# First layer's value projection as seven block products instead of eight, spread between the q and k projections

## The chip, the cores and the metric

The kernel runs on one core of one Trainium2 chip. The metric is the device time of one execution in microseconds (us); the median of two executions of the kernel before is 1992.58 us (1992.47 to 1992.68). A core has TensorE (PE, matrix products, with its weight loads shown apart as PEld), VectorE (DVE), ScalarE (ACT), GpSimd (POOL) and SyncE (SP, which issues most of the transfers). Each engine works through its own list of instructions in order.

## The reference, cut to what matters

Two layers over 256 tokens of width 2048, in float32. The change lies in the token mixer of the first layer (12 heads of width 128, plus 4 heads into 256 memory tokens):

```python
n = rms_norm(h, attn_norm[i])
z = n @ a_w_in[j]                                   # 2048 x (3*1536 + 512)
q, k, v, qm = jnp.split(z, [MIX_WIDTH, 2 * MIX_WIDTH, 3 * MIX_WIDTH], axis=-1)
mix = neighbourhood_attention(split_heads(q, 12), split_heads(k, 12), split_heads(v, 12), a_rpb[j])
km, vm = jnp.split(m @ w_mem_kv[i], 2, axis=-1)
cross = memory_attention(split_heads(qm, 4), split_heads(km, 4), split_heads(vm, 4))
h = h + jnp.concatenate([mix, cross], axis=-1) @ w_o[i]
n = rms_norm(h, mlp_norm[i])
h = h + jnp.square(jax.nn.relu(n @ w_up[i])) @ w_down[i]
```

The value projection is v = n @ (columns 3072 to 4607 of a_w_in): 256 x 2048 times 2048 x 1536.

## The kernel before

Every float32 operand of a large product is split into two rounded parts, hi (ScalarE copies it into the rounded type, L457) and lo (VectorE subtracts hi from the source, L458), and each product is three matmuls: hi times hi, hi times lo, lo times hi.

Weights come in chunks of 128 x 2048 floats (1 MB) into a ring: three buffers `raw` for what arrives, four `hi` and four `lo` tiles of half a chunk each (`new_half`). There are two kinds of chunk:

- kind "S" (`add_s`, `products`, L363): one head of 128 columns over all 2048 rows. The weights are the stationary operand, the 256 tokens are the moving one, so a matmul has 256 columns; 24 matmuls a half. The result is feature by token. Queries, keys and memory queries of the first layer and the MLP's up projection (`ps_u`) are of this kind.
- kind "M" (`add_m`, `m_products`, L340, L343, L344): 512 output columns over 512 rows. The tokens are stationary (two tiles of 128), the weights move, so a matmul has 512 columns; 12 matmuls a half. Values, w_o and the second layer's projections are of this kind.

`plan` is a list of chunks. `run_all` turns it into grains of half a chunk, calls the preparing stages a few grains ahead (`ahead`), and runs the grain; `later(n, fn)` puts a piece of work n grains after the present one. A scheduler then orders the instructions of each engine, from which the engines' lists come.

In the first layer the plan has four memory queries, and then three times: four chunks of values (512 columns, four heads) followed by the q and k chunks of those four heads. After each k chunk a narrow ("near") head starts: scores of 160 keys per token tile (`attend_near`), the turning of the probabilities through VectorE and SP's DMAs (`turned_near`), their split, and the product with the values (`attend3_near`). The memory heads go through `attend`, `turned`, `halved`, `attend3`. Values are read from PSUM, scaled and split by `put_values`.

The MLP already has a seven-product form for its down projection (`down_grains`): sums of the four weight blocks, made by VectorE and one accumulating DMA from the POOL queue (L1118 to L1124), and sums of the activations.

The starting places of operands are set by hand, in bytes: an S half starts `STILL_AT` = 64 bytes into its `hi` and `lo` tiles, an M half at byte 0, and a ring tile is longer than its 1024 floats by `LONGER`. The first S half behind an M half has its first 128 columns of lo elsewhere in the tile (`entered_half`, `Entered`).

Of the kernel before, what the change touches and what calls it, by code (L numbers as in the profile page):

```python
# [17 lines left out]
P = 128  # L18
# [41 lines left out]
LONGER = {"hi": 128, "lo": 128}  # L60
# [89 lines left out]

class Grain:


# [5 lines left out]
def encoder_kernel(ctx: ExitStack, tc: tile.TileContext, t: dict, out: bass.AP):  # L159
# [23 lines left out]
    def open_sums(layer=1):  # L183

        for x in ("acc", "att")[:: 1 if layer else -1]:
            setattr(at, x, opened(f"ps_{x}", space=bass.MemoryType.PSUM, bufs=4))

    def open_ring():
        at.ring = opened("ring")
        at.cat = opened("cat")  # L190

        for pool in (at.ring, at.cat):
            pool.tile([P, 64], F32, tag="pad", name="pad")
# [3 lines left out]

    open_sums()
    open_ring()
    open_work()  # L200

    first = const.tile([P, GAINS + NT * D], F32, name="first")
    gains, mem0 = first[:, :GAINS], first[:, GAINS:]
    h = mem0.rearrange("p (a b) -> p a b", a=NT)
# [3 lines left out]
    def load_mem(j):  # L210
        s = slice(GAINS + j * 512 if j else 0, GAINS + (j + 1) * 512)
        nc.sync.dma_start(first[:, s], t["mem_rest"][j - 1] if j else t["mem_first"])
# [26 lines left out]
    def gain(which, k):  # L239
        return gains[:, which * KT + k : which * KT + k + 1]  # L240
# [127 lines left out]
    def begin():  # L368

        box["memT"] = at.cat.tile([P, KT, 512], F32R, tag="cat", name="memT")  # L370
        tiles = {}
# [126 lines left out]
    def summed(ps, name, row, factor=1.0):  # L498

        s = at.work.tile([P, SEQ], F32, tag="sum_s", name=f"{name}_s")  # L500
        nc.vector.scalar_tensor_tensor(s, ps, factor, row, op0=ALU.mult, op1=ALU.mult)
        return s


    def attend(qT, kT):
# [19 lines left out]
        for s in range(NT):  # L525
            if box["layer"]:
                nc.scalar.activation(sc[:, s, :], sc[:, s, :], AF.Copy, scale=rs[:, s : s + 1])
            else:
                nc.vector.tensor_scalar(sc[:, s, :], sc[:, s, :], rs[:, s : s + 1], None, op0=ALU.mult)
        return sc  # L530

    def attend2(sc):
        pt = at.att.tile([P, NT, SEQ], F32, tag="att", name="pt_a")
        for s in range(NT):
            i = NT - 1 - s
            for k in range(NT):
                nc.tensor.transpose(pt[:, k, i * P : (i + 1) * P], sc[:, s, k * P : (k + 1) * P], ident)
        pT = at.work.tile([P, 2, NT, SEQ], F32R, tag="pT", bufs=2 + box["layer"], name="pT")
        return pT, split(pT[:, 0], pT[:, 1], pt)
# [20 lines left out]
    def turned(sc):  # L560
# [7 lines left out]
        pT = at.work.tile([P, 2, 4, NT, NT * 32], F32R, tag="pT", bufs=2 + box["layer"], name="pT_t")  # L568
# [55 lines left out]
    def attend3_near(pT, v, head, cat):  # L624
# [14 lines left out]
        y = at.work.tile([P, SEQ], F32, tag="av_s", name="av_s")  # L639
# [71 lines left out]
    def head_of(v, hd):  # L711
        return lambda part, kt: v[:, part, kt, hd * HD : (hd + 1) * HD]
# [32 lines left out]
    def vm_done(layer):  # L745
        def f(w):
# [4 lines left out]
            for i in range(NT):  # L751
                v = at.work.tile([P, 2, 512], F32R, tag="pT", name="vm_w")
# [22 lines left out]
    mem_sq = at.work.tile([P, 512], F32, tag="b_o", bufs=3, name="mem_sq")  # L775
# [20 lines left out]
    def x_load():  # L796
        box["xT"] = []
        for a in range(2):
            y = at.work.tile([P, 8, SEQ], F32, tag="l4", name="xT")
            pin(nc.sync.dma_start(y.rearrange("p a b -> p (a b)"), t["xT"][:, a * XW // 2 : (a + 1) * XW // 2]))  # L800
            box["xT"].append(y)
# [15 lines left out]
    def x_norm(j):  # L817
        if j == 0:
            box["nT"] = wide("nT0", 480)
        for k in (2 * j, 2 * j + 1):  # L820
            split_pair(box["nT"], box["xT"][k // 8][:, k % 8, :], G_A0, k)
# [21 lines left out]
    def a_k_done(hd):  # L843
        def f(w):
# [5 lines left out]
            attention([(box.pop(("q", hd)), k, b, head_of(box["v", hd // GH], hd % GH), hd, box["cat"])], 1,  # L850
                      steps=(0, 1, 3, 4 if hd == NH - 1 else 8 if hd % GH == GH - 1 else 7))
        return f

    def a_qm_done(hd):
        def f(w):
# [6 lines left out]
            attention([(q, box["km"][:, hd, :], None, head_of(box["vm"], hd), NH + hd, box["cat"])], 1)  # L862
# [30 lines left out]
    def o_done(layer, nb):  # L893
# [41 lines left out]
        def f(w):  # L935
            if nb == 0:
                closed("work")
# [288 lines left out]
    def plain_grains(layer, nb, at_chunk):  # L1226
# [19 lines left out]
        def begin():  # L1246
            if nb == REST[0]:
                closed("ps_sums")
                open_sums(layer)
# [295 lines left out]
    for j in range(8):  # L1545
        later(24 + j, x_norm, j)
    later(28, x_stats)
# [28 lines left out]
def m_chunks(w):  # L1576

    k, n = w.shape
    x = w.reshape(k // D, 4, 4, P, n // 512, 512).transpose(0, 4, 1, 3, 2, 5)
    return np.ascontiguousarray(x).reshape(-1, P, CH)  # L1580
# [118 lines left out]
```

## Time and profile before

| what | value |
|---|---|
| median of the executions | 1992.58 us |
| the profiled execution's own time | 1992.26 us |
| its span in the profile | 1990.3 us, 32806 instructions |
| TensorE busy | 1981.8 us, 100%, 12838 matmuls |
| VectorE busy | 1716.2 us, 86% |
| ScalarE busy | 1340.0 us, 67% |
| GpSimd busy | 138.3 us, 7% |
| moved by DMA | 448.52 MB, mean 225 GB/s |

The span is what the profiler saw from the first instruction to the last; the execution's own time is 1.96 us longer. A matmul's bar in the profile is 276 to 278 ns long at 256 columns and about 390 ns at 512, but the next one starts long before it ends, so the cost of a matmul is read from one start to the next, not from its bar. For VectorE and ScalarE a bar also overlaps its neighbour a little when both wait for nothing.

### The profile page before, as it was taken

The numbers are of one execution on the slowest core, as the hardware profiler recorded it, in microseconds if no ns is written. First come the engines' busy times: TensorE is split into PE (matmuls) and PEld (weight loads), VectorE is DVE, ScalarE is ACT, GpSimd is POOL, SyncE is SP. The second block draws the span as 40 slices with busy tenths as digits, with TensorE's granted clock in tenths as the row PEclk, the third lists the DMA queues.
The fourth block names the chain that finished last, engine by engine and source line by source line (L and its number), as shares of the span: only waits on it lengthen the run. The fifth ranks groups of instructions, "written<-read, shape, count | busy, mean of one in ns | idle before, by whom it ended". The sixth has DMA issues, their size and how long they took to land.

```text
span 1990.3 us, 32806 instructions
## 1 busy us (share of the span) xinstructions
PE 1981.8 (100%) x12838; PEld 1800.0 (90%) x12838; DVE 1716.2 (86%) x2131; ACT 1340.0 (67%) x1892; POOL 138.3 (7%) x179
## 2 busy tenths in 40 slices
PE   9999999999999999999999999999999999999998
PEld 8999999899999999999998888889999999999997
DVE  7777777588898999999999778788998999999998
ACT  6655555477777777777766658677776777777674
POOL 0000000000000000000000001000000000000000
PEclk9999999999999999999999999999999999999999
DMA  8856655767777777777766765667777777777772
GB/s 293 321 194 202 206 189 184 271 191 234 239 230 227 232 236 238 230 228 235 216 229 198 259 223 182 211 213 251 236 224 236 226 226 238 234 238 229 225 236 105
DMA packets 117339, 448.52 MB, mean 225 GB/s; under 512 B 24640, under 2 KB 49984, under 8 KB 69824
## 3 DMA queue, kind: packets, MB, share of 16 engines
q1 hardware_dynamic: 99168, 415.12, 59.6%
q0 software_dynamic: 17728, 30.78, 9.7%
q8 instruction: 101, 1.65, 0.3%
q10 hardware_dynamic: 288, 0.52, 0.1%
q14 instruction: 54, 0.44, 0.1%
HBM read 397.78 MB, written 4.19 MB: 202 GB/s over the span
## 4 chain that ended last, share of the span: by engine, by line
PE 99%; issue 0%; DMA 0%; ACT 0%; DVE 0%; DVEq 0%; POOLq 0%; POOL 0%; SPq 0%; ACTq 0%
PE ps_u L363 35%; PE ps_s L363 10%; PE p L1152 9%; PE p L1150 9%; PE p L1153 9%; PE ps_m L344 8%; PE ps_m L340 8%; PE ps_m L343 8%; PE sc_ps L514 0%; PE av L655 0%; PE sc_ps L513 0%; PE sc_ps L515 0%; PE av L654 0%; PE av L656 0%; PE av L630 0%
## 5 line engine op out<-in xcount | busy, mean ns | idle before, releaser
L363 PE MATMUL ps_u<-hT,uh 128*128 128x256 f32 x3812 | 663.9, 276 | 0.0
L363 PEld LDWEIGHTS ps_u<-hT,uh 128*128 128x128 f32 x3812 | 579.1, 188 | 5.5
L363 PE MATMUL ps_u<-hT,ul 128*128 128x256 f32 x1960 | 541.7, 276 | 0.0
L457 ACT ACTIVATE uh<-raw_U 128x1024 fp32r<-128x1024 f32 x262 | 276.8, 1058 | 210.1 <-PE ps_u L363 194.7
L363 PEld LDWEIGHTS ps_u<-hT,ul 128*128 128x128 f32 x1960 | 368.2, 188 | 0.0
L458 DVE TENSOR_TENSOR lo<-raw,hi 128x1024 fp32r<-128x1024 f32 (+1 forms) x215 | 254.0, 1187 | 93.6 <-ACT hi L457 92.7
L458 DVE TENSOR_TENSOR ul<-raw_U,uh 128x1024 fp32r<-128x1024 f32 x262 | 318.1, 1217 | 17.3 <-ACT uh L457 17.3
L458 DVE TENSOR_TENSOR tl<-t,th 128x2048 fp32r<-128x2048 f32 x116 | 265.5, 2289 | 71.0 <-ACT th L457 70.6
L457 ACT ACTIVATE hi<-raw 128x1024 fp32r<-128x1024 f32 (+1 forms) x215 | 222.1, 1039 | 140.7 <-PE ps_m L344 72.9
L457 ACT ACTIVATE th<-t 128x2048 fp32r<-128x2048 f32 x116 | 222.7, 1919 | 118.0 <-PE p L1153 114.9
L458 DVE TENSOR_TENSOR bl<-b,bh 128x1536 fp32r<-128x1536 f32 x116 | 203.1, 1751 | 0.0
L1150 PE MATMUL p<-th,a_s 128*128 128x512 f32 x464 | 181.2, 391 | 0.0
L1152 PE MATMUL p<-tl,a_s 128*128 128x512 f32 x464 | 181.0, 390 | 0.0
L1153 PE MATMUL p<-th,a_s 128*128 128x512 f32 x464 | 180.5, 389 | 0.0
L1119 POOL DMA_DIRECT2D t<-b x116 | 100.7, 868 | 1142.0 <-ACT t L1118 1059.7
L457 ACT ACTIVATE bh<-b 128x1536 fp32r<-128x1536 f32 x116 | 172.3, 1486 | 7.9
L363 PE MATMUL ps_s<-nT,hi 128*128 128x256 f32 x896 | 154.7, 277 | 0.0
L1153 PE MATMUL p<-bh,a_s 128*128 128x512 f32 x348 | 136.2, 391 | 0.0
L1152 PE MATMUL p<-bl,a_s 128*128 128x512 f32 x348 | 135.7, 390 | 0.0
L363 PEld LDWEIGHTS ps_s<-nT,hi 128*128 128x128 f32 x896 | 135.6, 188 | 0.1
L1150 PE MATMUL p<-bh,a_s 128*128 128x512 f32 x348 | 135.4, 389 | 0.0
L363 PE MATMUL ps_s<-nT,lo 128*128 128x256 f32 x448 | 124.1, 277 | 0.0
(303 smaller groups left out, 3585.6 us busy)
## 6 DMA issues: line engine op xcount, KB each, us to landing
raw_U<-in_w_up SPq DMA_DIRECT2D x128, 1024.0 KB, 6.0
b<-in_w_pair SPq DMA_DIRECT2D x116, 1024.0 KB, 5.8
raw<-in_w_o SPq DMA_DIRECT2D x32, 1024.0 KB, 5.1
t<-b POOLq DMA_DIRECT2D x116, 256.0 KB, 5.2
raw<-in_w_b SPq DMA_DIRECT2D x21, 1024.0 KB, 5.7
raw<-in_w_av SPq DMA_DIRECT2D x12, 1024.0 KB, 5.0
raw<-in_w_aq SPq DMA_DIRECT2D x12, 1024.0 KB, 4.9
raw<-in_w_ak SPq DMA_DIRECT2D x12, 1024.0 KB, 5.0
```

The costliest lines, as they stand in the source:

```text
L340: first = nc.tensor.matmul(ps, ah, hi[:, s], start=st, stop=False)
L343: nc.tensor.matmul(ps, ah, lo[:, s], start=False, stop=False)
L344: final = nc.tensor.matmul(ps, al, hi[:, s], start=False, stop=sp)
L363: ins = nc.tensor.matmul(ps, x, acts[:, k, part], start=k == n == 0, stop=k == KT - 1 and n == 2)
L457: first = nc.scalar.activation(dst_hi, src, AF.Copy)
L458: return first, nc.vector.tensor_tensor(dst_lo, src, dst_hi.bitcast(F32), op=ALU.subtract)
L1119: nc.gpsimd.dma_start(s[:, 3, :], b[:, 1, :], accum_op=ALU.add)
L1150: ins = nc.tensor.matmul(ps, a[:, 0, ai, :], hi[:, s], start=begins, stop=False)
L1152: nc.tensor.matmul(ps, a[:, 0, ai, :], lo[:, s], start=False, stop=False)
L1153: nc.tensor.matmul(ps, a[:, 1, ai, :], hi[:, s], start=False, stop=ends)
```

## The change

The values of four heads (512 columns) are now computed from 2 x 2 blocks: the two token tiles of 128, pairs of 128-row blocks of the weights, and halves of 256 columns. Seven products per pair of blocks, each 128 tokens by 256 columns, take the place of eight. That needs sums of the activations (`x_sums`, made once, in `left`, in part of `cat` and in the room of h, which is loaded a second time after the values are done) and sums of the weights (`value_grains`: one ScalarE copy, two VectorE additions and two accumulating DMAs from the POOL queue for each of the 12 chunks). The seven sums stand in four PSUM banks, and seven VectorE additions (`values_done`, three times) make the four blocks of values from them.

The plan no longer has values in blocks of four chunks. One value grain follows each of the 28 projection chunks (four memory queries, then q and k of each head) from the third on, which is the third memory query, and two follow n = 4, 5 and 6 (the first head's q and k and the second head's q), until the 24 grains are used up. Beside them the q and k products alternate between the two halves of one PSUM bank (`"turns"`); PSUM then has five `acc` and three `att` banks in the first layer, four and four before. The ring tiles become shorter to make room: `hi` by 112 floats, `lo` by 64. Several work tiles lose a buffer. The memory heads' probabilities are scaled by ScalarE instead of VectorE, and their steps stand further apart.

```diff
-LONGER = {"hi": 128, "lo": 128}
+LONGER = {"hi": 16, "lo": 64}
...
-        for x in ("acc", "att")[:: 1 if layer else -1]:
-            setattr(at, x, opened(f"ps_{x}", space=bass.MemoryType.PSUM, bufs=4))
+        for x, n in (("acc", 5 - layer), ("att", 3 + layer))[:: 1 if layer else -1]:
+            setattr(at, x, opened(f"ps_{x}", space=bass.MemoryType.PSUM, bufs=n))
...
+            if place == "turns":
+                if "turns" not in box:
+                    box["turns"] = [0, at.acc.tile([P, 512], F32, tag="acc", name="ps_s")]
+                box["turns"][0] += 1
+                w.ps = box["turns"][1][:, box["turns"][0] % 2 * SEQ :][:, :SEQ]
+                return
...
+    def x_sums(c):
...
+        d = at.work.tile([P, 2, 4, P], F32, tag="pT", bufs=1, name="x_d")
+        for n, a, b, op in ((0, x[:, :, 0], x[:, :, 2], ALU.subtract), (1, x[:, :, 0], x[:, :, 1], ALU.add),
+                            (2, d[:, :, 0], x[:, :, 1], ALU.add), (3, x[:, :, 3], d[:, :, 2], ALU.subtract)):
+            nc.vector.tensor_tensor(d[:, :, n], a, b, op=op)
+        split(res[:, :, 0], res[:, :, 1], d)
...
-    def a_v_done(g):
-        def f(w):
-            box["v", g] = values("l4", "va")
-            put_values(box["v", g], w.ps, box["x_col"])
-        return f
+    PARTS = (("p3", "p1", "p2", "p7"), ("p6", "p4", "p5"))
...
+        def pre():
+            b = own["b"].rearrange("p (a b) -> p a b", a=4)
+            s = own["t"] = at.spare.tile([P, 4, 512], F32, tag="sums", name="v_t")
+            nc.scalar.activation(s[:, 2:4, :], b[:, 2:4, :], AF.Copy)
+            nc.vector.tensor_tensor(s[:, 0, :], b[:, 3, :], b[:, 0, :], op=ALU.add)
+            nc.gpsimd.dma_start(s[:, 3, :], b[:, 1, :], accum_op=ALU.add)
+            nc.vector.tensor_tensor(s[:, 1, :], s[:, 0, :], b[:, 1, :], op=ALU.add)
+            nc.gpsimd.dma_start(s[:, 2, :], s[:, 1, :], accum_op=ALU.add)
+
+        def prep(n):
+            b, s = own["b"], own["t"].rearrange("p a b -> p (a b)")
+            for m, src in enumerate(((s[:, 512 : 1536], s[:, 1536:]) if n else (b[:, :HALF], b[:, HALF : 1536], s[:, :512]))):
+                if m < 2:
+                    own[n, m] = new_half("S")
+                at_ = slice(0, src.shape[-1]) if m < 2 else slice(512, HALF)
+                split(*(x[:, at_] for x in own[n, min(m, 1)]), src)
...
+        def run(n):
...
+                        for part, x, st, sp in ((0, hi, begin and half == 0, False), (0, lo, False, False),
+                                                (1, hi, False, end)):
...
+                            ins = nc.tensor.matmul(ps, ah, x[:, s], start=st, stop=sp, skip_group_check=True)
...
+    def values_done(g):
...
+        nc.scalar.activation(c[:, 0, 0], p["p1"], AF.Copy)
+        for d, x, y, op in ((c[:, 1, 0], p["p2"], c[:, 0, 0], ALU.add), (c[:, 1, 1], p["p6"], c[:, 0, 0], ALU.subtract),
+                            (c[:, 0, 1], c[:, 1, 1], p["p7"], ALU.subtract), (c[:, 0, 0], c[:, 0, 1], p["p4"], ALU.add),
+                            (c[:, 0, 1], p["p5"], c[:, 0, 1], ALU.subtract),
+                            (c[:, 1, 1], c[:, 1, 1], p["p5"], ALU.subtract), (c[:, 1, 1], c[:, 1, 1], p["p3"], ALU.add)):
+            nc.vector.tensor_tensor(d, x, y, op=op)
...
-    for hd in range(NMH):
-        add_s(t["w_aqm"][hd], get("nT"), a_qm_done(hd))
-    for g in range(NH // GH):
-        add_m([t["w_av"][g * 4 + c] for c in range(4)], parts_of("nT"), a_v_done(g))
-        for hd in range(g * GH, (g + 1) * GH):
-            add_s(t["w_aq"][hd], get("nT"), a_q_done(hd))
-            add_s(t["w_ak"][hd], get("nT"), a_k_done(hd))
+    CHUNKS = (2, 0, 1, 3)
+    with_values = [x for g in range(NH // GH) for n, c in enumerate(CHUNKS) for x in value_grains(g, c, n == 0, n == 3)]
+    projections = [(t["w_aqm"][hd], a_qm_done(hd)) for hd in range(NMH)]
+    for hd in range(NH):
+        projections += [(t["w_aq"][hd], a_q_done(hd)), (t["w_ak"][hd], a_k_done(hd))]
+    for n, (src, done) in enumerate(projections):
+        add_s(src, get("nT"), done, "turns" if with_values else None)
+        for _ in range((n > 1) + (n in (4, 5, 6))):
+            if with_values:
+                plan.append(with_values.pop(0))
```

What this makes of the lists of instructions is seen at two places. On TensorE, where the first values are computed, behind a memory head (`av`, `sc_ps`), before and then now; `ps_m` and `ps_v` are the values' sums, `nT` the normed tokens, `left` their sums:

```order
L656 MATMUL av<-pT_t,vm 128x256
L340 MATMUL ps_m<-hi,nT_920 128x512
L343 MATMUL ps_m<-lo,nT_920 128x512
L344 MATMUL ps_m<-hi,nT_920 128x512
L340 MATMUL ps_m<-hi,nT_920 128x512
L343 MATMUL ps_m<-lo,nT_920 128x512
```

```order
L540 MATMUL sc_ps<-km,qmT 128x256
L928 MATMUL ps_v<-hi,left 128x256
L928 MATMUL ps_v<-lo,left 128x256
L928 MATMUL ps_v<-hi,left 128x256
L928 MATMUL ps_v<-hi,nT_925 128x256
L928 MATMUL ps_v<-lo,nT_925 128x256
```

288 matmuls of 512 columns are gone, 504 of 256 columns stand in their place, in groups of 24 and 18 between the q and k products (`ps_s`), which before came without a break.

On VectorE, where the last two memory heads (`nm`, `sc_t`, `pT_t`) are worked on while the first values are prepared, before:

```order
L524 RECIPROCAL rs<-sm 128x2
L529 TENSOR_SCALAR sc<-sc,rs 128x256 x2
L566 STREAM_TRANSPOSE sc_t<-sc 128x2x4x32 x2
L458 TENSOR_TENSOR lo<-raw,hi 128x1024 x2
L458 TENSOR_TENSOR cat_1154<-av,cat_1154 128x256
L458 TENSOR_TENSOR pT_t<-pT_t 128x512
L314 TENSOR_TENSOR lo<-raw,hi 128x128
L314 TENSOR_TENSOR lo<-raw,hi 128x896
L458 TENSOR_TENSOR lo<-raw,hi 128x1024 x2
```

and now (`v_t` are the weight sums, `x_d` and `cat<-x_d` the last of the activation sums):

```order
L894 TENSOR_TENSOR v_t<-raw 128x512
L332 TENSOR_TENSOR lo<-raw,hi 128x896
L588 STREAM_TRANSPOSE sc_t<-sc 128x2x4x32 x2
L896 TENSOR_TENSOR v_t<-v_t,raw 128x512
L544 TENSOR_REDUCE nm<-sc_ps 128x2
L526 SCALAR_TENSOR_TENSOR qm_s<-ps_s,x_row 128x256
L483 TENSOR_TENSOR cat_1177<-x_d,cat_1177 128x2x512
L483 TENSOR_TENSOR lo<-raw,hi 128x1024
L549 RECIPROCAL rs<-sm 128x2
L483 TENSOR_TENSOR qmT<-qm_s,qmT 128x256
L483 TENSOR_TENSOR lo<-raw,hi 128x1024
L588 STREAM_TRANSPOSE sc_t<-sc 128x2x4x32 x2
```

The memory heads, the sums of activations and weights and the splits of three kinds of chunk now share one stretch of VectorE's list.

More of the change, by code (lines that the diff above doesn't have):

```diff
@@ L370, in begin @@
         box["memT"] = at.cat.tile([P, KT, 512], F32R, tag="cat", name="memT")
+        later(1, lambda: nc.scalar.activation(gains, first[:, LEFT : LEFT + GAINS], AF.Copy))
         tiles = {}
@@ new lines, in values_done @@
+    def values_done(g):
+        p = {name: box["v_ps"][bank][:, half * SEQ : (half + 1) * SEQ] for name, (bank, half) in PLACES.items()}
+        c = at.work.tile([P, NT, 2, SEQ], F32, tag="pT", bufs=1, name="v_c")
+        nc.scalar.activation(c[:, 0, 0], p["p1"], AF.Copy)
[4 more added lines that the diff above has]
+            nc.vector.tensor_tensor(d, x, y, op=op)
+        box["v", g] = values("l4", "va")
+        put_values(box["v", g], [c[:, i].rearrange("p a b -> p (a b)") for i in range(NT)], box["x_col"])
+        if g == NH // GH - 1:
+            h_load()
@@ L936, in f @@
             if nb == 0:
+                if not layer:
+                    closed("spare")
                 closed("work")
@@ L1544, in encoder_kernel @@
     later(21, x_load)
[L1545 to L1547 removed]
+    for n, j in enumerate((4, 5, 0, 1, 2, 3, 6, 7)):
+        later(24 + n, x_norm, j)
+    for n, c in zip((28, 30, 32, 35), CHUNKS):
+        later(n, x_sums, c)
+    later(26, x_stats)
     run_all()
```

130 lines of the change are left out of this document (100 added, 30 removed).

## The prediction

> **What bounds the kernel now.** I read the busy times first, then the slices, then the chain of work that ended last.
>
> ```profile
> PE 1981.8 (100%) x12838; PEld 1800.0 (90%) x12838; DVE 1716.2 (86%) x2131; ACT 1340.0 (67%) x1892; POOL 138.3 (7%) x179
> PE   9999999999999999999999999999999999999998
> DVE  7777777588898999999999778788998999999998
> PEclk9999999999999999999999999999999999999999
> PE 99%; issue 0%; DMA 0%; ACT 0%; DVE 0%; DVEq 0%; POOLq 0%; POOL 0%; SPq 0%; ACTq 0%
> ```
>
> TensorE is busy throughout, its granted clock never drops, and the chain is 99% TensorE. So only two things move the time: what a matmul costs from one start to the next, and a new wait of TensorE. VectorE is the next engine, 70 to 80% busy in the slices of the first layer's projections (a slice is 49.8 us). The busy times of each engine in three stretches of that stage say it more closely (sum, then the number of instructions):
>
> ```profile
> core 0: us, PE busy (x) PEld busy (x) DVE busy (x) ACT busy (x) POOL busy (x), PEclk, DMA share, GB/s
> 94.00:330.00 236.00, 236.00 (x1769) 224.29 (x1768) 178.11 (x340) 123.81 (x212) 10.97 (x22) 1.00 0.61 202
> 105.50:156.50 51.00, 51.00 (x353) 47.06 (x351) 37.90 (x61) 27.54 (x48) 0.00 (x0) 1.00 0.58 193
> ```
>
> From 94 to 330 us TensorE has no gap, VectorE works 178.1 us of 236, ScalarE 123.8. The transfers are at 0.61 of their engines, so loading the same weights in another order, and h twice (two transfers more on SP's list of some 600), I cost at nothing; a late 1 MB chunk would show as an idle `hi` copy.
>
> **The change part by part: the matmuls.** First the chain, then TensorE's own rows, give the cost from start to start.
>
> ```profile
> 213.54 14.52 PE ps_s L363 x128
> ...
> 204.70 0.39 PE L340 MATMUL ps_m<-hi,nT 128*128 128x512 f32 x1
> ...
> 211.95 0.39 PE L344 MATMUL ps_m<-hi,nT 128*128 128x512 f32 x1
> ...
> L340 PE MATMUL ps_m<-hi,nT 128*128 128x512 f32 x96 | 37.5, 390 | 0.0
> L343 PE MATMUL ps_m<-lo,nT 128*128 128x512 f32 x96 | 37.4, 390 | 0.0
> L344 PE MATMUL ps_m<-hi,nT 128*128 128x512 f32 x96 | 37.6, 391 | 0.0
> ```
>
> 128 matmuls of 256 columns in 14.52 us are 113.4 ns each. The two 512-column rows are 32 matmuls apart: 7.25 us / 32 = 226.6 ns, twice 113.3, so two narrow ones cost what a wide one does. Removed are the three groups, 288 x 226.6 ns = 65.3 us; with slower ones at each switch of kind the starts add up to 65.7. Added are 504 (12 chunks, 42 each) x 113.4 = 57.2 us. **Gain 8.5 us.** The other bound is the nearest row of a product of the tokens-stationary kind that really has 256 columns, the kernel's last products:
>
> ```profile
> 1977.26 0.28 PE L343 MATMUL ps_m<-ul,a_s 128*128 128x256 f32 x1
> ...
> 1981.94 0.28 PE L343 MATMUL ps_m<-l_p,a_p 128*128 128x256 f32 x1
> ```
>
> Those are 39 matmuls apart, 4.68 / 39 = 120.0 ns; 504 x 120.0 = 60.5, a gain of 5.2. I take 8.5 here and put the difference into the next term, because I think I know where it comes from.
>
> [...]
>
> **The starting places.** In the kernel before, the `hi` tiles lie (1024 + 128) x 4 = 4608 bytes apart, 36 times 128. Now it is (1024 + 16) x 4 = 4160, 32.5 times 128, so every second `hi` tile starts 64 bytes off its old place modulo 128. Before, every q and k matmul reads its moving operand 64 bytes, modulo 128, from the next one's weights, and the last products, 120.0 ns each, read them 0 apart. Counting addresses through the new program, 544 of 1695 narrow pairs of the S kind and 177 of 498 value pairs become 0 apart, and 483 of 1758 wide pairs 64 apart. At 120.0 − 113.4 = 6.6 ns that is 3.6 + 1.2 = 4.8 us, and another 0 to 3.2 if the wide ones suffer too: bounds 0 to 8. But one row speaks against laying it all on the place:
>
> ```profile
> 422.18 17.91 PE ps_u L363 x152
> ```
>
> These 152 narrow matmuls also have operands 64 apart and still take 117.8 ns, so only 120.0 − 117.8 = 2.2 ns is surely left for the place: 721 x 2.2 = 1.6 us. Between 1.6 and 4.8 I take **+2.6 us**, nearer to the 117.8, since that row stands in a far longer run than the 4.7 us of the last products.
>
> **VectorE's share.** What an operation costs when VectorE waits for nothing is read from starts:
>
> ```profile
> 601.13 1.08 DVE L458 TENSOR_TENSOR a_s<-c,a_s 128x896 fp32r<-128x896 f32 x1
> 602.13 1.75 DVE L458 TENSOR_TENSOR bl<-b,bh 128x1536 fp32r<-128x1536 f32 x1
> 603.80 0.69 DVE L1122 TENSOR_TENSOR t<-b 128x512 f32<-128x512 f32 x1
> 604.40 1.22 DVE L458 TENSOR_TENSOR ul<-raw_U,uh 128x1024 fp32r<-128x1024 f32 x1
> 605.54 0.68 DVE L1123 TENSOR_TENSOR t<-t,b 128x512 f32<-128x512 f32 x1
> 606.14 1.22 DVE L458 TENSOR_TENSOR ul<-raw_U,uh 128x1024 fp32r<-128x1024 f32 x1
> ...
> 173.08 0.41 DVE L501 SCALAR_TENSOR_TENSOR q_s<-ps_s,x_row 128x256 f32<-128x256 f32 x1
> 173.41 0.47 DVE L590 TENSOR_REDUCE nm<-sc 128x2 f32<-128x320 f32 x1
> ```
>
> So 896 elements take 1.00 us, 512 take 0.60, 1024 take 1.14, 256 about 0.33; on the same line 128 would be 0.20, and an entered half (128 + 896) 1.20. By the two lists the change takes away 30 splits of 1024 (−34.2) and the scaling of the memory heads (−2.4, ScalarE does it now); it adds 18 entered halves (21.6), per value chunk one raw split of 512, one split of a sum of 1024 and two of 512 and two additions of 512 (12 x 4.14 = 49.7), 21 additions that make the values (7.0), and the activation sums (16 x 0.33 + 4 x 1.14 = 9.9); splitting the normed tokens in pairs saves 1.1. Together +50.5 us: 178.1 + 50.5 = 228.6 against TensorE's 236 − 8.5 = 227.5. ScalarE gets some 45 more and stays under 75%.
>
> This is not even. Where one grain follows each projection VectorE's list has 16.0 us of work per head, TensorE 138 matmuls (15.6 us) and 1.1 for the head itself, 16.7, so it holds. Between the first value product and the end of the doubled places (n = 4, 5, 6) TensorE has 51 us of work, and VectorE's list holds 63: 13 splits of 1024, 14 of 512 and 6 entered halves (30.4), 8 weight sums (4.8), activation sums (6.4), the values' additions (3.0), near heads and q, k (5.4), and most of the four memory heads (12.8), whose steps and scaling before are these:
>
> ```profile
> L566 DVE STREAM_TRANSPOSE sc_t<-sc 128x256 f32<-128x256 f32 x8 | 4.6, 614 | 0.0
> L519 DVE TENSOR_REDUCE nm<-sc_ps 128x2 f32<-128x512 f32 x4 | 2.8, 688 | 1.4 <-PE sc_ps L515 1.4
> L458 DVE TENSOR_TENSOR pT_t<-pT_t 128x512 fp32r<-128x512 f32 x4 | 2.8, 692 | 4.4 <-ACT pT_t L457 4.4
> L501 DVE SCALAR_TENSOR_TENSOR qm_s<-ps_s,x_row 128x256 f32<-128x256 f32 x4 | 1.7, 418 | 0.5 <-PE ps_s L363 0.5
> L529 DVE TENSOR_SCALAR sc<-sc,rs 128x256 f32<-128x256 f32 x8 | 2.4, 347 | 0.0
> ```
>
> Less 0.08 us of overlap a bar, a head's two transposes, maximum, split of pT_t, and three steps of 256 elements (qm_s and two more) are 2 x 0.53 + 2 x 0.61 + 3 x 0.34 = 3.3 us, four heads 13.2. The 63 us are 12 too many. VectorE enters with a lead, which the ring bounds: a tile becomes free, ScalarE copies, VectorE subtracts, TensorE uses it.
>
> ```profile
> 99.77 1.06 ACT L457 ACTIVATE hi<-raw 128x1024 fp32r<-128x1024 f32 x1 [1.60 <-PE ps_s L363]
> 100.87 1.23 DVE L458 TENSOR_TENSOR lo<-raw,hi 128x1024 fp32r<-128x1024 f32 x1 [0.56 <-ACT hi L457]
> ```
>
> This tile is ready at 102.1 and first used at 107.8: a lead of 5.7 us. Some of the 63 us (sums made before the first value product, memory steps with room behind them) can slip to either side of the stretch, some 2 us each way. 12 − 5.7 − 2 leaves **+4 us** of waiting, bounds 0 (all of it slips) and 12 (no lead). A lag is made up later at 0.7 us a head, but what TensorE has waited is lost.
>
> The second accumulating transfer of a chunk waits for the first VectorE additions and is waited for by the sums' splits. The MLP's like transfer:
>
> ```profile
> L1119 POOL DMA_DIRECT2D t<-b x116 | 100.7, 868 | 1142.0 <-ACT t L1118 1059.7
> ...
> t<-b POOLq DMA_DIRECT2D x116, 256.0 KB, 5.2
> ```
>
> Issue 0.87, landing 5.2, then a ScalarE copy: some 7 us. VectorE's list leaves 6.6 us of other work for it at the two tightest chunks, so it costs nothing or some tenths, part of the 4 us; with landing times of 9 us it would be 2 more a chunk there. The new turns in one bank cost nothing while 48 products, 5.4 us, stand between two writes of one half and a reader like the 0.41 us `q_s` ends in time.
>
> **Sum:** −8.5 + 2.6 + 4.0 = −1.9 us. The profiled execution took 1992.26, so 1990.4; its median is 0.32 above it, hence 1990.7.
>
> **The rivals.** First, the gain comes through nearly whole: places free, VectorE's list slipping enough. −8.5 + 0 to 4 gives 1984 to 1988. For it: 13.1 of the 51 us VectorE was idle in that stretch before, and its lag may stay inside the ring; against it: 228.6 us of work for 227.5.
>
> Second, the places are free but VectorE stalls as above: −8.5 + 4 = 1988.1. The row for it is the 117.8 ns at the unchanged place, against it 113.4 and 120.0 at one clock of 1.00. [...]
>
> Third, on the slower side, VectorE stalls TensorE in full at the doubled places: each half tile comes late because the lists interleave memory heads, sums and splits, so the lead is spent by the second value chunk; 8 to 12 us, and places at 2.6. −8.5 + 2.6 + 8 to 12 = +2 to +6, with places at 8 up to +11.5: 1994.5 to 2004. It decides as soon as stall and places together exceed 8.5 us.
>
> **How the numbers follow.** Forecast (1988.5 to 1994) 0.45; first rival 0.27; second 0.08; third 0.20. The range 1984 to 1999.5 leaves out the far half of the third rival and what lies under the first. About 2% (39.9 us) is what a measurement of this kernel can tell from no change; no case comes near it on either side: faster 0.005, same 0.985, slower 0.01.
>
> **What the profile after would show.** Right on the first term: `ps_v` at 113 to 114 ns from start to start where both operands are 64 apart. On places: q and k products of every second `hi` tile at up to 120 ns, in alternating stretches. On VectorE: busy over 95% between 105 and 160 us, and idle time of TensorE there put down to VectorE's `lo`, 4 us in all, little later on. The prediction is wrong if TensorE has no gap there, if it has gaps in every head, or if the granted clock leaves 1.00.

## The result, and the profile after

The changed kernel takes 2062.15 us, against 1992.58 before: 69.6 us more, a ratio of 1.0349 (95% interval 1.0305 to 1.0394). The forecast was 1990.7 with a range of 1984 to 1999.5. The same lines of the changed kernel's page that were shown of the kernel before:

```profile
span 2060.5 us, 33506 instructions
PE 2008.9 (97%) x13054; PEld 1827.4 (89%) x13054; DVE 1765.9 (86%) x2234; ACT 1386.3 (67%) x1972; POOL 161.7 (8%) x203
PE   9987888999999999999999999999999999999998
DVE  6786777858889999999999778778989999999997
PEclk9998989999999999999999999999999999999999
PE 88%; DMA 4%; DVE 4%; ACT 2%; issue 1%; SPq 0%; DVEq 0%; POOLq 0%; POOL 0%; ACTq 0%
```

The chain is no longer TensorE alone: transfers, VectorE and ScalarE hold 10% of it. The holes are in slices 3 to 7 (a slice is now 51.5 us), the stage of the first layer's projections, and the granted clock dips there (0.94 on average from 94 to 390 us). The same stage by busy times, and what TensorE waited for in it (total, times, longest):

```profile
core 0: us, PE busy (x) PEld busy (x) DVE busy (x) ACT busy (x) POOL busy (x), PEclk, DMA share, GB/s
94.00:390.00 296.00, 257.06 (x1990) 251.59 (x1989) 223.68 (x438) 163.45 (x282) 33.18 (x47) 0.94 0.63 190
105.00:160.00 55.00, 44.66 (x342) 43.54 (x342) 43.88 (x76) 34.41 (x68) 3.50 (x4) 0.93 0.57 169
...
PE sc_ps L606 <- ACT kT L482: 12.2, 5, 3.8
PE ps_s L381 <- DVE qm_s L526: 7.7, 3, 4.9
PE ps_s L381 <- DVE lo L332: 7.2, 3, 4.6
PE av L676 <- ACT pT_t L482: 7.1, 2, 5.2
```

VectorE's 223.7 us are close to the 228.6 that the prediction worked out, but it needed 296 us for them: 76% busy, as before (178.1 of 236). So it was not short of time on the whole, and from 105 to 160 us, where the prediction looked for over 95%, it was busy for 80% (43.9 of 55 us). It waited too, in a circle with the others. Reading every start of a matmul from the first q-kind product on the tokens to the last k product gives this account of the stage (in us). "Full rate" is 113.4 ns for each narrow matmul and 226.6 for each wide one, "heads" what the attention matmuls took, "idle" what the times from start to start with a gap in them took over full rate, "half clock" what starts about 213 ns apart cost over 113.4, "slower starts" the smaller excesses:

| kernel | stage | full rate | heads | idle | half clock | slower starts |
|---|---|---|---|---|---|---|
| before | 235.0 | 217.6 | 16.2 | 0.0 | 0.0 | 1.3 |
| changed | 293.2 | 209.5 | 20.2 | 41.8 | 14.9 | 6.9 |
| load5 | 273.6 | 209.5 | 18.5 | 29.8 | 8.0 | 7.8 |
| all_four | 247.8 | 209.5 | 18.8 | 11.3 | 3.3 | 4.9 |
| m_only | 237.6 | 209.5 | 17.3 | 2.9 | 2.9 | 5.1 |
| m_load8 | 260.2 | 209.5 | 18.4 | 18.0 | 9.5 | 4.7 |

At full rate the matmuls gained 8.1 us, close to the forecast 8.5; waiting and the clock behind each wait took 56.7, slower starts 5.6, the attention matmuls (partly at half clock) 4.0. Ahead of the stage the changed kernel lost 3.0 us, behind it, up to the last matmul, 8.6.

**How one wait comes about.** The kernel before, the load of a q chunk (SP's queue) and its first reader:

```profile
226.76 0.33 SPq L273 DMA_DIRECT2D raw<-in_w_aq  x1
...
239.54 1.05 ACT L457 ACTIVATE hi<-raw 128x1024 fp32r<-128x1024 f32 x1
```

12.8 us lie between them. In the changed kernel, a value chunk's load and first reader, and then the loads of two q chunks, with what followed the second:

```profile
222.74 0.33 SPq L888 DMA_DIRECT2D raw<-in_w_av  x1
...
244.61 1.06 ACT L893 ACTIVATE v_t<-raw 128x1024 f32<-128x1024 f32 x1 [0.30 <-DVE lo L483]
...
231.22 1.49 SPq L291 DMA_DIRECT2D raw<-in_w_aq  x1
...
238.06 1.06 ACT L330 ACTIVATE hi<-raw 128x1024 fp32r<-128x1024 f32 x1 [1.77 <-DMA raw<-in_w_aq]
...
249.83 0.33 SPq L291 DMA_DIRECT2D raw<-in_w_aq  x1
...
257.23 1.06 ACT L330 ACTIVATE hi<-raw 128x1024 fp32r<-128x1024 f32 x1 [6.74 <-DMA raw<-in_w_aq]
258.32 1.29 DVE L332 TENSOR_TENSOR lo<-raw,hi 128x128 fp32r<-128x128 f32 x2 [3.80 <-ACT hi L330]
258.67 0.58 PE L381 MATMUL ps_s<-nT,lo 128*128 128x256 f32 x1 [4.61 <-DVE lo L332]
```

The value chunk's load is given out 8 grains ahead, a projection chunk's together with its first split, 3 ahead. So the value chunk sits 21.9 us in one of the three `raw` buffers before anything reads it (24 to 31 us for the others of the stage), and two buffers are left for q and k. A q load can go out only when VectorE's last `lo` of an older chunk frees a buffer, 5 to 7 us ahead of use (in some cases 0.2 to 0.7 us after the buffer is free, behind a head's transfers on SP's list). While it travels, ScalarE stands at `hi` for 6.7 us, VectorE behind it 3.8, TensorE 4.6, and nobody works ahead.

The largest row of the waits, `kT`, is for the most part the same wait. Two of its five, 3.8 us each, come about like this one: the head's keys are ready for ScalarE at 301.3 us, but a q chunk's `hi` stands ahead of them in its list and waits for its transfer.

```profile
303.24 1.06 ACT L330 ACTIVATE hi<-raw 128x1024 fp32r<-128x1024 f32 x1 [3.33 <-DMA raw<-in_w_aq]
304.20 0.40 ACT L482 ACTIVATE kT<-k_s 128x256 fp32r<-128x256 f32 x1
...
304.66 0.34 PE L606 MATMUL sc_ps<-kT,qT 128*128 128x160 f32 x1 [3.79 <-ACT kT L482]
```

### The profile page after: what moved, and what is told of

Its sections match the earlier page's. It is cut to its first block, busy times and chain, and to the rows that moved or that the text cites. A ratio compares the mean times of both kernels' runs of the same rounds, so it can differ in the third digit from the quotient of the medians.

```text
span 2060.5 us, 33506 instructions
## 1 busy us (share of the span) xinstructions
PE 2008.9 (97%) x13054; PEld 1827.4 (89%) x13054; DVE 1765.9 (86%) x2234; ACT 1386.3 (67%) x1972; POOL 161.7 (8%) x203
## 4 chain that ended last, share of the span: by engine, by line
PE 88%; DMA 4%; DVE 4%; ACT 2%; issue 1%; SPq 0%; DVEq 0%; POOLq 0%; POOL 0%; ACTq 0%
PE ps_u L381 34%; PE p L1285 9%; PE p L1287 9%; PE p L1288 9%; PE ps_m L358 6%; PE ps_m L361 6%; PE ps_m L362 6%; PE ps_s L381 5%; DMA raw<-in_w_aq 2%; PE ps_v L928 1%; DVE lo L483 1%; DVE lo L332 1%; ACT hi L482 0%; DMA pT_n<-sc_t 0%; DMA raw<-in_w_aqm 0%
## 5 line engine op out<-in xcount | busy, mean ns | idle before, releaser
L483 DVE TENSOR_TENSOR lo<-raw,hi 128x1024 fp32r<-128x1024 f32 (+1 forms) x197 | 225.2, 1153 | 84.5 <-ACT hi L482 83.6
L482 ACT ACTIVATE hi<-raw 128x1024 fp32r<-128x1024 f32 (+1 forms) x197 | 196.4, 1007 | 117.0 <-PE ps_m L362 77.0
L381 PE MATMUL ps_s<-nT,hi 128*128 128x256 f32 x896 | 167.2, 291 | 5.4 <-DVE qm_s L526 5.4
L381 PEld LDWEIGHTS ps_s<-nT,hi 128*128 128x128 f32 x896 | 143.6, 199 | 5.8 <-ACT hi L482 5.0
L381 PE MATMUL ps_s<-nT,lo 128*128 128x256 f32 x448 | 131.0, 292 | 12.3 <-DVE lo L332 7.2
```

What stands on the lines that cost most here:

```text
L381: ins = nc.tensor.matmul(ps, x, acts[:, k, part], start=k == n == 0, stop=k == KT - 1 and n == 2)
L482: first = nc.scalar.activation(dst_hi, src, AF.Copy)
L483: return first, nc.vector.tensor_tensor(dst_lo, src, dst_hi.bitcast(F32), op=ALU.subtract)
```

## The experiments

Each was timed beside the kernel before (1992.2 to 1992.8 us). Most undo something in the changed kernel; two change the kernel before instead, and the last six are a version with the new matmuls but without the sums and additions, and what is put back on it.

**load5.** Value chunks are loaded later.

```diff
-        return [Grain(lambda: run(0), None, load, pre, lambda: prep(0)),
+        return [Grain(lambda: run(0), None, load, pre, lambda: prep(0), (5, 5, 3)),
```

> The changed kernel with the value chunks' loads given out 5 grains ahead of their products instead of 8 (their weight sums stay at 5, their splits at 3). Ring theory: a value chunk now lies 22 to 30 us in one of the three raw buffers between its load's issue and its first reader, so q and k chunks are loaded only 5 to 7 us before ScalarE wants them; given out later, the value chunk holds its buffer for under 20 us, q's load is issued 9 us or more ahead, TensorE's idle time between 100 and 390 us falls from 34 us to under 12, the clock stays nearer to 1.00, and the time is 2000 to 2020 us. VectorE theory (its longer list is what comes late): nothing moves by more than 5 us, 2057 to 2067.

2042.56 us, 19.6 less. In the steady part q's load now goes out 12 to 15 us ahead of its reader, value chunks stand 11 to 14 us. The direction is the ring's, the size is not: 29.8 us of idle time stay, and the waits have another name.

```profile
PE ps_s L381 <- DVE k_s L526: 8.7, 8, 2.2
PE av L676 <- ACT pT_t L482: 7.4, 2, 5.1
PE ps_s L381 <- DVE qm_s L526: 7.3, 3, 5.1
```

One of them, on TensorE and VectorE:

```profile
213.83 0.28 PE L381 MATMUL ps_s<-nT,lo 128*128 128x256 f32 x1
...
214.15 0.42 DVE L526 SCALAR_TENSOR_TENSOR k_s<-ps_s,x_row 128x256 f32<-128x256 f32 x1
...
214.63 0.39 PE L381 MATMUL ps_s<-nT,lo 128*128 128x256 f32 x1 [0.52 <-DVE k_s L526]
```

The k product ends, VectorE reads it, and only then the next product starts, though it writes the other half of the bank. In the program the first matmul of a product waits for the read of the one before it, so the two halves count as one.

**resident.** No value chunk is loaded.

```diff
-            own["b"] = at.ring.tile([P, CH], F32, tag="raw", bufs=3, name="raw")
-            nc.sync.dma_start(own["b"], t["w_av"][g * 4 + c])
+            own["b"] = box["left_room"].bitcast(F32)    # in pre()
```

> The changed kernel with the values' weights read from a tile that lies in SBUF already (the sums of activations of one chunk) in place of the 12 loaded chunks; all matmuls, splits, sums and accumulating transfers of the values stay, their 12 loads and their use of the raw buffers are left out, so the values are not the reference's. Ring theory: the raw buffers serve q and k alone, q's load is issued 12 us or more ahead, TensorE's idle time between 100 and 390 us falls from 34 us to under 6, and the time is 1988 to 2003. VectorE theory: VectorE has the same list, so the gaps stay and the time is 2045 to 2062.

2038.09 us. Both theories missed: taking the value chunks out of the ring gives 24.1 us, and no more, because the waits for `k_s`, `qm_s` and `pT_t` take over.

**places_before.** The kernel before, with other tile lengths alone.

```diff
-LONGER = {"hi": 128, "lo": 128}
+LONGER = {"hi": 16, "lo": 64}
```

> The kernel before with the changed kernel's LONGER (hi 16, lo 64 floats), so that every second hi tile starts 64 bytes off, and nothing else. Places theory: narrow matmuls of the first layer in every second tile go from 113 to 118 ns, 3 to 8 us in the projections, and as much again in the memory's, w_o's and second layer's chunks: 1997 to 2008. Ring and VectorE theory: the places are not the cause, 1992 to 1995.

2006.09 us, 13.4 more (ratio 1.0068, 1.0051 to 1.0085), with no gap. The chain's longest piece in the stage, to be read beside the 14.52 us for as many matmuls before:

```profile
218.88 15.06 PE ps_s L363 x128
```

117.7 ns each for 113.4. Of the 13.4 us, 2.6 fall ahead of the first attention matmul, 6.3 between it and the last k product, the rest on w_o and the second layer. Halves in tiles that kept their place are slow as well (117.1 ns on average, 119.1 in the moved ones).

**hi32.** Every hi tile starts alike modulo 128 bytes again.

```diff
-LONGER = {"hi": 16, "lo": 64}
+LONGER = {"hi": 32, "lo": 64}
-        at.ring.tile([P, 64], F32, tag="pad", name="pad")
```

> The changed kernel with hi tiles longer by 32 floats instead of 16 (4224 bytes apart, 33 times 128, so that every tile starts alike) and the ring's pad of 64 floats gone to make room. Places theory: the narrow matmuls go from 118 back to 113 ns where TensorE does not wait, but the waits come from the ring, so the time falls by 3 to 10 us: 2052 to 2059. If places cost nothing: 2060 to 2064.

2056.96 us, 5.2 less. The memory's narrow products are back at 113.7 ns on average, but the wide ones stay at 229 to 232 against 226.6, and in the stage the narrow ones at 116.6. The shorter tiles cost 13.4 us in the kernel before and 8.5 in m_places (below), so equal places modulo 128 undo a part of that at most.

**load5_two_banks.** As load5, and q and k alternate between two banks.

```diff
+                    box["turns"] = [0] + [at.acc.tile([P, 512], F32, tag="acc", name="ps_s") for _ in range(2)]
...
+                w.ps = box["turns"][1 + box["turns"][0] % 2][:, :SEQ]
...
-    PLACES = {... "p6": (2, 0), "p4": (2, 1), "p5": (3, 0)}
+    PLACES = {... "p6": (2, 0), "p4": (2, 1), "p5": (2, 1)}
```

> The value chunks' loads 5 grains ahead, and the q and k products alternate between two whole PSUM banks instead of the two halves of one; to free a bank the product p5 is summed into p4's half, so the values are not the reference's, while every matmul and every VectorE read stays. Bank theory: in the changed kernel a product waits for VectorE's read of the product just before it (q_s, k_s, qm_s), although that lies in the other half; in load5 TensorE waits 16.7 us for those three, 11 gaps. With two banks they go, and with them part of the stretches at half clock: 2018 to 2030, against 2042.6 for load5. If the halves of a bank were independent already: 2038 to 2045.

2024.95 us, 17.6 under load5, as the bank theory said; the waits for `q_s`, `k_s` and `qm_s` are gone from the list.

**pT2.** Two buffers for tag pT; the third chunk's activation sums are left out for the room.

```diff
-        pT = at.work.tile([P, 2, 4, NT, NT * 32], F32R, tag="pT", bufs=1 + 2 * box["layer"], name="pT_t")
+        pT = at.work.tile([P, 2, 4, NT, NT * 32], F32R, tag="pT", bufs=2 + box["layer"], name="pT_t")
```

> The changed kernel with two buffers for the tiles of tag pT (the memory heads' turned probabilities, the activation differences, the values being put together), as the kernel before had for the probabilities; the room comes from the activation sums of the third chunk, left out as in all_four. Single buffer theory: TensorE's two waits for pT_t (7.1 us, the longest 5.2) go, with some half clock behind them, 2048 to 2055. If the ring sets these too: 2057 to 2062.

2050.32 us, 11.8 less, as expected; no wait for `pT_t` is left. Part of it may come from the sums left out, 2.5 us of VectorE's work by the prediction's prices.

**all_four** has later loads, two banks, two pT buffers and `LONGER` of 128 and 128.

> Loads 5 grains ahead, two banks for q and k (p5 summed into p4's half), two buffers for the tiles of tag pT, and hi and lo tiles longer by 128 floats as in the kernel before. The room comes from the activation sums of the third chunk, which are left out (the first chunk's are read in their place; 2.5 us of VectorE's work goes with them), so the values are not the reference's. Theory that ring, bank, single buffer and places together are the cause: what is left is the gain of 8.5 us and little waiting, 1984 to 1996. VectorE theory: its list is too long for the stage, 10 us and more of waiting for lo stay, 2000 to 2015.

2008.00 us: 54.2 less than the changed kernel, still 15.7 over the kernel before. The number lies where the VectorE theory put it, but not for its reason, 10 us and more of waiting for `lo`: there are 2.7 us of it, and no single wait of TensorE in the stage is over 1.3 us. VectorE has little room, 92.3 of the 100 us in this stretch; that this is what the rest comes from is not shown.

```profile
PE ps_s L381 <- DVE lo L332: 2.7, 6, 0.8
...
200.00:300.00 100.00, 98.38 (x826) 96.94 (x825) 92.33 (x194) 66.47 (x115) 17.33 (x24) 1.00 0.73 216
```

**all_no_sums** replaces the weight sums as well.

```diff
-            nc.scalar.activation(s[:, 2:4, :], b[:, 2:4, :], AF.Copy)
-            nc.vector.tensor_tensor(s[:, 0, :], b[:, 3, :], b[:, 0, :], op=ALU.add)
-            nc.gpsimd.dma_start(s[:, 3, :], b[:, 1, :], accum_op=ALU.add)
-            nc.vector.tensor_tensor(s[:, 1, :], s[:, 0, :], b[:, 1, :], op=ALU.add)
-            nc.gpsimd.dma_start(s[:, 2, :], s[:, 1, :], accum_op=ALU.add)
+            nc.scalar.activation(s, b, AF.Copy)
```

> As all_four, and the weight sums replaced by one ScalarE copy of the chunk, so that 24 VectorE additions (14.4 us) and 24 accumulating transfers are left out. VectorE theory: 8 us or more less than all_four. If VectorE keeps up in all_four: within 3 us of it.

2002.82 us, 5.2 less, between the two theories.

Three more undo one thing each in the changed kernel, to see whether the causes add up. **own_buffer** gives the value chunks a raw buffer of their own (`tag="raw_v"`, in the room of the third chunk's activation sums, which are left out):

> The changed kernel, loads 8 grains ahead as in it, but the value chunks have a raw buffer of their own, so that q and k chunks have the three of the ring to themselves. The room comes from the activation sums of the third chunk, left out as before (2.5 us of VectorE's work with them), so the values are not the reference's. Ring theory: q's load is issued 11 us or more before ScalarE wants it, the idle time of 35 to 42 us falls by as much as with later loads (load5) or with a resident tile, 2033 to 2045. VectorE theory: under 5 us, 2057 to 2062.

2028.61 us, 33.5 less, more than any other single edit and below the range; most of the waiting that is left is the bank's (`k_s`, `qm_s` and `q_s`: 13.9 us). **two_banks** is the banks' edit without later loads:

> The changed kernel with two PSUM banks for the q and k products (p5 summed into p4's half, so the values are not the reference's), loads 8 grains ahead as in it. Bank theory: TensorE's waits for q_s, k_s and qm_s (10.5 us, 7 gaps) go with some half clock. If the causes simply add up, the 17.6 us that two banks gave behind load5 come here too, 2042 to 2048; if the ring makes the same gaps again where the bank no longer does, 5 to 12 us, 2050 to 2057.

2045.33 us, 16.8 less, so the ring does not eat it. **no_sums** is the sums' edit alone:

> The changed kernel with the weight sums replaced by one ScalarE copy, so that 24 additions on VectorE (14.4 us) and 24 accumulating transfers are left out, and the values are not the reference's. The step on VectorE in the prediction (its longer list is what TensorE waits for): 10 us or more faster, under 2052. Ring and bank theory: VectorE's list matters little as long as the loads come late, 2 to 8 us, 2054 to 2060.

2047.03 us, 15.1 less: the sums, 24 additions on VectorE and 24 transfers, do matter, against the 2 to 8 us of the ring and bank theory. Undone one at a time, loads (33.5 with an own buffer), banks (16.8), sums (15.1), pT (11.8) and hi's places (5.2) give 82.4 us together, more than there is to undo (the 69.6 lost and the 8.1 that the matmuls gained, 77.7). They overlap; the reading that fits is that each lengthens the same circle of `raw` buffer, load, ScalarE, VectorE and TensorE.

**interleaved_before.** The kernel before, with its eight-product value chunks put between the q and k chunks.

```diff
...
+    for n, (src, done) in enumerate(projections):
+        add_s(src, get("nT"), done)
+        if with_values and (n in (3, 5) or n >= 4 and n % 2 == 0):
+            plan.append(with_values.pop(0))
```

> The kernel before with its 12 value chunks (eight products, 512 columns, unchanged) no longer in blocks of four but one by one between q and k chunks: behind the fourth memory query, behind the next three chunks, then behind every second one. No sums, no shared bank, places as before. If alternating two kinds of product costs TensorE time by itself (the first matmuls behind each switch are slower): 1 to 5 us more, 1993.5 to 1998. If the order alone makes loads or splits late: gaps and more than that. Ring theory: each chunk is loaded right ahead of its splits, as before, so no gaps.

1992.64 us, ratio 1.0000 (0.9991 to 1.0010), TensorE without a gap. Alternating whole chunks of the two kinds cost nothing here by itself.

**m_only** goes the other way: the new matmuls in the new order, with the loads 5 grains ahead, two banks, two pT buffers and the old tile lengths, and without the sums and additions. The splits of the seven parts stay, so VectorE works 195.6 us in the stage, 18.3 more than in the same stage before (177.3).

```diff
-            return box["left", c][:, q, part, SUM[name], :]
+            return box["nT"][:, (2 * c + q) * 2 + SUM[name] % 2, part * SEQ + SUM[name] // 2 * P :][:, :P]
...
-            b, s = own["b"], own["t"].rearrange("p a b -> p (a b)")
+            b = s = own["b"]
...
+        put_values(box["v", g], box["v_ps"][:NT], box["x_col"])
```

> Only the matmuls of the change: 504 narrow ones for 288 wide ones, in the new plan between q and k chunks, loads 5 grains ahead, two banks (p5 summed into p4's half), two pT buffers, tiles as long as in the kernel before. Left out: all sums of activations and weights, the accumulating transfers, and the additions that make the values (two of the sums are scaled and split in their place), so the values are not the reference's. If the first term of the prediction holds on the chip: 8.5 us under the kernel before, 1982.5 to 1986, with no gap. If the new order itself makes gaps even with VectorE's work as before: 1990 or more.

1997.54 us, ratio 1.0026 (1.0016 to 1.0037): a miss. The 8.1 us at full rate are there (209.5 for 217.6 in the account), but one head's start still waits 1.4 us, half clock follows it (2.9 us), narrow starts stay slow (3.8 us; the value products take 117.0 ns on average for 113.4), and some 4 us go ahead of the stage and in the MLP. So even free of its sums this arrangement does not beat the kernel before, and the experiments point to no version that does.

On m_only each suspect was then put alone. **m_load8**: `(8, 5, 3)` again.

> As m_only, with the value chunks' loads 8 grains ahead as in the change. Ring theory as a cause by itself: q and k are again loaded 5 to 8 us ahead of use and TensorE waits, 8 to 20 us over m_only. If late loads hurt only where VectorE has no room left: under 4 us.

2018.36 us, 20.8 more, and the wait has the ring's name:

```profile
PE ps_s L381 <- DVE lo L332: 12.6, 8, 2.8
...
ACT hi L330 <- DMA raw<-in_w_aq: 14.5, 5, 4.2
```

But it is not the changed kernel's load alone. Without weight sums the splits of a chunk's second grain, too, read the `raw` buffer, so it comes free 3 grains later: held for 8 grains in m_load8, 5 in m_only, 5 in the changed kernel (whose second grain reads the sums) and 2 in load5. From the load to the last read, in the steady part, that is 39 to 44 us, 29 to 31, 30 to 37 and 19 to 22. So m_only holds a buffer about as long as the changed kernel and shows no wait of TensorE for `lo` over 0.2 us in the stage: that hold by itself cost next to nothing there, and a hold 3 grains longer cost 20.8 us.

**m_sums**: the weight sums again.

> As m_only, with the weight sums as in the change (24 additions on VectorE, 24 accumulating transfers, one buffer for the sums, splits from it). VectorE theory: 14.4 us more work for it and a chain of two transfers a chunk behind its in-order list make gaps, 4 to 12 us over m_only. If they hide: within 2 us of m_only.

2004.88 us, 7.3 more, with the `raw` buffers free earlier again (17 to 20 us after the load). **m_one_bank**: the halves of one bank again.

> As m_only, with q and k in the two halves of one PSUM bank as in the change (values then in their four banks, p5 in its own half). Bank theory as a cause by itself: each product waits for VectorE's read of the one before unless a value grain of 2 us or more lies between, 3 to 10 us over m_only. If the read comes in time wherever VectorE has room: under 2 us.

2003.51 us, 6.0 more, again with the bank's name:

```profile
PE ps_s L381 <- DVE k_s L526: 7.2, 8, 1.6
PE ps_s L381 <- DVE qm_s L526: 1.7, 2, 1.2
```

**m_one_pT**: one buffer for pT again.

> As m_only, with one buffer for the tiles of tag pT as in the change (the memory's values on their way out and the memory heads' turned probabilities). Single buffer theory as a cause by itself: a head's probabilities cannot be turned before the one ahead has used its own, TensorE waits for pT_t, 3 to 8 us over m_only. If there is room: under 2 us.

2000.31 us, 2.8 more, just under the range; one wait:

```profile
PE av L676 <- ACT pT_t L482: 2.4, 1, 2.4
```

**m_places**: `LONGER = {"hi": 16, "lo": 64}` again.

> As m_only, with hi tiles longer by 16 floats and lo by 64 as in the change. Places theory: as in the kernel before with those lengths (13.4 us), 8 to 14 us over m_only, without a new gap. If the slower starts came only with the old order: under 4 us.

2006.06 us, 8.5 more. Nearly all that the two traces differ by (6.6 of 6.7 us) lies ahead of the stage and behind it.

From below, then: m_only is 4.7 us over the kernel before, places add 8.5, weight sums 7.3, the bank 6.0, the single buffer 2.8. That is 29.3 of 69.6 us. The other 40.3 belong to what was not put on m_only alone (activation sums, the values' additions, their share of VectorE) and to the causes working on each other, the early loads among them: 19.6 to 33.5 us in the changed kernel, next to nothing with the same hold in m_only. How much belongs to which stays open.

## Why the prediction was wrong

**The matmuls** (8.5 us): right at full rate, where narrow starts cost half of wide ones (113.4 ns for 226.6), 57.2 us for 65.3. But the value products do not keep that rate: at m_only's 117.0 ns (starts at half clock left aside) 504 of them are 59.0 us, and the gain is 6.3, between the prediction's two bounds.

**The starting places** (+2.6, bounds 0 to 8): it was right that they cost something, but the size was off, and its mechanism is a part of it at most. It counted pairs in the projections alone, though the same tiles carry the memory's, w_o's and the second layer's chunks, and it took only the flipped pairs as slower, while halves that kept their place slow down too, and equal places modulo 128 (hi32) win back 5.2 us only. Measured 13.4 us in the kernel before and 8.5 in m_only. The rival that had them free falls with it: the lengths alone changed the time, with no wait. What makes the starts slower is not shown here.

**VectorE's share** (+4.0, bounds 0 to 12): its added work was sized well (223.7 us busy for 228.6), and the weight sums with their transfers, put on m_only, cost 7.3. The step that failed is the one that took the lists as if only their sum and a lead of 5.7 us counted. The idle time is 41.8 us in a stage in which VectorE is busy for no larger share than before, 76%.

**"Loading the same weights in another order I cost at nothing"**: this is the largest single miss. The prediction read the transfers' share of 0.61 and not the buffer that a transfer needs. The sign it named, an idle `hi` copy, is there (6.7 us). The change gives out a value chunk's load 5 grains earlier than a projection's, from the same three buffers. In the changed kernel later loads undo 19.6 us of it and a buffer of its own 33.5; m_only, with a hold as long, shows that it takes the other delays to make it cost that.

**"The new turns in one bank cost nothing"**: wrong. It compared reader and next writer of one half; the wait is for the whole bank, so the cover is not 48 products but whatever lies between two neighbouring products, often nothing. 6.0 us alone, 17.6 behind load5.

**Fewer buffers and the clock** were not priced at all. The single pT buffer is 2.8 us alone and 11.8 in the changed kernel. And each longer wait was charged again at half clock, 14.9 us together, where the prediction said only that the clock might leave 1.00.

The third rival had the sign and the place of the first gaps, but its end (2004) stood on the same sum. Gaps in every head and a granted clock under 1.00 were named as what would prove the forecast wrong, and both are there; VectorE over 95% busy from 105 to 160 us is not.

## What to carry to other kernels

Before pricing a reordered load at nothing, write down for each buffer of its pool when it is taken and when it comes free: a load given out early takes a buffer from the others (a buffer of its own won back 33.5 us in the changed kernel, at a DMA share of 0.63). Take a tile's two halves as one for waits until a trace shows otherwise (two banks won back 16.8 us), and count every stage that uses a tile whose length changes. When a tuned pipeline loses several small covers at once, undoing one in the slow version can give more than it costs alone (banks 16.8 for 6.0 us, the pT buffer 11.8 for 2.8). Putting each on a version without gaps shows what it costs alone, if that version keeps the rest as it was, such as how long a buffer is held.

## What the runs showed of the hardware

In the changed kernel the matmuls ran at half rate behind the longer waits of TensorE, starts 213 ns apart for 113.4, until 3.2 to 6.2 us after the wait. TensorE's starts behind a wait of 2.28 us, and the granted clock (the figure ahead of the last two) right behind that wait, around it, and around the 4.61 us wait:

```profile
134.34 0.39 PE L381 MATMUL ps_s<-nT,lo 128*128 128x256 f32 x1 [2.28 <-DVE qm_s L526]
...
137.04 0.41 PE L381 MATMUL ps_s<-nT,lo 128*128 128x256 f32 x1
137.25 0.63 PE L381 MATMUL ps_s<-nT,hi 128*128 128x256 f32 x2
137.68 0.41 PE L381 MATMUL ps_s<-nT,lo 128*128 128x256 f32 x1
...
135.00:138.00 3.00, 3.00 (x16) 3.00 (x16) 1.95 (x4) 1.29 (x4) 0.00 (x0) 0.50 0.73 134
130.00:140.00 10.00, 7.72 (x53) 7.51 (x52) 6.97 (x13) 6.72 (x13) 1.74 (x2) 0.83 0.59 113
250.00:260.00 10.00, 5.39 (x41) 5.18 (x40) 5.57 (x12) 3.16 (x5) 1.06 (x2) 0.89 0.81 238
260.00:270.00 10.00, 10.00 (x68) 10.00 (x68) 6.00 (x14) 3.78 (x10) 0.00 (x0) 0.77 0.37 123
```

The starts from 137.04 to 137.68 are 213 ns apart, at a granted clock of 0.50. The slow stretch ends some 4 us behind the wait. From 260 to 270 TensorE has no gap and still gets only 0.77. In this trace waits of 1.85, 2.26 and 2.28 us were each enough, and two of 1.6 us, 0.8 us apart, together; one of 1.39 us was not, and those under 1 us were followed by one start of 221 to 226 ns where a q, k or memory query product came next.

The other surprise is a second, slower rate of the matmuls at full clock. With the shorter tiles of places_before, narrow starts take some 118 ns for 113.4 in the tiles that kept their place, too; the first half of a run of q and k products still takes 113.7, the fifth, in the same `hi` tile, 117.8. And it comes without the shift. These are the memory's narrow products in m_only and in m_load8, whose tiles are as long as in the kernel before and whose granted clock is 1.00 in this stretch:

```profile
14.93 13.07 PE ps_s L381 x111
...
14.94 13.15 PE ps_s L381 x116
```

That is 117.7 ns each in one and 113.4 in the other. So the tile lengths change the rate but are not all that does. What else does is not shown.
